# Layer 2's output projection and gate: high weights against high and low activations in one 512-column product, and a new order of the program

## The chip, the cores and the metric

The kernel runs on one core of a Trainium2 chip. The metric is the device time of one execution in microseconds (us). The engines are TensorE (PE), VectorE (DVE), ScalarE (ACT), GpSimd (POOL) and SyncE (SP), which issues most DMAs.

## The reference

Two residual layers over one sequence of T = 256 tokens with D = 1024 channels. Layer 1 mixes tokens by MoBA attention, layer 2 by NSA (compressed, selected and window branches). What surrounds the attention is the same in both, here cut to what matters:

```python
h = rms_norm(x, gain)
q, k, v, z = split(h @ w_in)
o = merge_heads(attention(q, k, v)) * silu(z)
x = x + o @ w_out                                        # output projection: 1024 x 1024
gate = sigmoid(rms_norm(x, ple_gain) @ w_gate)           # gate: 1024 x 1024
x = x + gate * (p @ w_proj)                              # p: 256 channels per token
```

All inputs are float32 and the result has to be as exact as float32 products make it.

## The kernel before

**Products.** x is kept transposed in SBUF as `xT`, 128 channels on the partitions, 8 tiles of channels (k), 256 tokens. Each float32 matrix is split in two fp32r parts, hi and lo, and a product is the sum of three: hi weights with hi activations, hi weights with lo activations, lo weights with hi activations. `split_act` (L498) makes the two parts of an activation tile, ACT the hi part (`ah`), DVE the lo part (`al`), each a tile of its own.

**Units.** Weights come in granules of 128 x 1024 numbers (512 KB): a DMA into `raw`, an ACT copy into `hi` (L494), a DVE subtraction into `lo` (L495). Class `Unit` (L512) covers 512 output columns. For projection, gate and the silu path z, the weights are stationary and the 256 tokens move (`feat`): for each k and each of four 128-row output tiles, three matmuls of 256 columns (`mul`, L531). Two output tiles share one PSUM bank of 512 columns. A granule has two k. Steps are named by layer (n for layer 2), kind, half of the output and granule: `w:no0.1` loads and splits granule 1 of the first half of layer 2's projection, `no0.1` multiplies with it, `no0/0` multiplies the remaining granules for one bank, `no0>0` evacuates that bank.

**Tail.** `tail` (L695) builds these steps for each layer and the evacuations: `add_out` (L725) adds a bank of 512 columns to two tiles of xT with one DVE instruction; `gate` (L731) multiplies by the reciprocal norm (DVE), takes a tanh (ACT), and with two more DVE instructions multiplies by the projected p and adds to xT. In the second half of the gate each output tile has a bank of its own and is evacuated alone (256 columns), the very last in two halves of 128 tokens, each followed by its store.

**Order.** `PROGRAM` (L25) is a string of step names. Class `Plan` (L106) records the instructions of the steps in that order and assigns each engine a static order by list scheduling: the index in the string is the priority, and tables of costs, latencies and a `MARGIN` decide what may go first. All engine instructions are issued by one line of `emit`, so the profile shows nearly every row as L396. Each engine runs its list strictly in that order; a step early in the string can only pass a later one if its inputs come first. The program is: loads of x and the first key weights, layer 1's input products and attention (A, S, T, V steps), its z, projection and gate; then the same for layer 2, whose attention has steps such as `2S0`, `3T3` (softmax and transposes of a head group), `3B` (its masks), `nx.k` (gated attention output, split).

Of the kernel before, what the change touches and what calls it, by code (L numbers as in the profile page):

```python
# [8 lines left out]
F32R = mybir.dt.float32r  # L9
AF = mybir.ActivationFunctionType  # L10
OP = mybir.AluOpType
AX = mybir.AxisListType

P = 128
T = 256
D = 1024
KT = 8
# [2 lines left out]
SWITCH, POW = 150.0, 2300.0  # L20
NRAW, NHI, NLO, NPT, NA = 5, 5, 5, 9, 9
WARM = 16
MARGIN = 100.0

PROGRAM = ("x0 w:c0 x2 c0 x1 w:c1 c1 x3 w:c2 c2 x4 w:c3 w:c4 x5 c3 w:c5 w:k.0 x6 w:c6 consts x7 k.0 w:c7 c4 w:k.1 c5 "  # L25
# [22 lines left out]

STORES = 5

# [8 lines left out]
class View:  # L59


    def __init__(self, tile_, ap, steps=()):
        self.tile, self.ap, self.steps = tile_, ap, steps
# [354 lines left out]
def trunk(ctx: ExitStack, tc: tile.TileContext, a, out):  # L418
# [3 lines left out]
    nc = Plan(tc.nc, {"sb": sb, "psum": psum})  # L422
# [8 lines left out]
    consts, wpool, apool, work = Pool(1), Pool(5), Pool(NA), Pool(2)  # L431
# [8 lines left out]
    xT = consts.tile([P, KT, T], F32, name="xT")  # L440
# [55 lines left out]
        return (hi.rearrange("p (a b) -> p a b", a=shape[0]), lo.rearrange("p (a b) -> p a b", a=shape[0]))  # L496

    def split_act(src, gain=None, either=False):  # L498
        hi = apool.tile([P, T], F32R, tag="ah", name="ah")
        lo = apool.tile([P, T], F32R, tag="al", name="al")  # L500
        if gain is None:
            nc.scalar.activation(hi, src, AF.Copy)
            nc.vector.tensor_tensor(lo, src, hi.bitcast(F32), op=OP.subtract)
        else:
            if either:
                nc.copy(hi, src, gain)
            else:
                nc.scalar.activation(hi, src, AF.Copy, scale=gain)
            nc.vector.scalar_tensor_tensor(lo, src, gain, hi.bitcast(F32), op0=OP.mult, op1=OP.subtract)
        return hi, lo  # L510

    class Unit:  # L512

# [15 lines left out]
            self.w[g] = split(self.src[g], (self.kg, self.n))  # L529

        def mul(self, w, j, k, b, ms=(0, 1), cols=None, parts=(0, 1, 2)):  # L531
            (wh, wl), (xh, xl) = w, self.xs[k]
            first, last = k == 0, k == self.nk - 1
            if self.feat:
                for m in ms:
                    o = self.ps[2 * b + m] if self.apart else self.ps[b][:, m * T:m * T + T]
                    s = slice((2 * b + m) * P, (2 * b + m + 1) * P)
                    nc.tensor.matmul(o, wh[:, j, s], xh, start=first and (self.apart or m == 0), stop=False,
                                     skip_group_check=True)
                    nc.tensor.matmul(o, wh[:, j, s], xl, start=False, stop=False, skip_group_check=True)  # L540
                    nc.tensor.matmul(o, wl[:, j, s], xh, start=False, stop=last, skip_group_check=True)
            else:
                c0, c1 = cols or (0, self.n)
                o, s = self.ps[b][:, c0:c1], slice(b * P, b * P + P)
                for i in parts:
                    x, y = ((xh, wh), (xl, wh), (xh, wl))[i]
                    nc.tensor.matmul(o, x[:, s], y[:, j], start=first and c0 == i == 0, stop=last and i == 2,
                                     skip_group_check=True)
# [12 lines left out]
        def steps(self, name):  # L561

            for g in range(self.granules):
                todo[f"w:{name}.{g}"] = lambda g=g: self.weights(g)
                if g < self.whole:
                    todo[f"{name}.{g}"] = lambda g=g: self.step(g)
            for i in range(len(self.parts)):
                todo[f"{name}/{i}"] = lambda i=i: self.part(i)
            return self

    todo = {}
# [115 lines left out]
    def evac_z(zz, u, i, m, norm):  # L687
        zr = tmp("zr").rearrange("p (a b) -> p a b", a=2)
        nc.vector.tensor_tensor(zr, u.ps[i].rearrange("p (a b) -> p a b", a=2),
                                norm.bc[:, None, :].to_broadcast([P, 2, T]), op=OP.mult)  # L690
        th = tmp("th").rearrange("p (a b) -> p a b", a=2)
        nc.scalar.activation(th, zr, AF.Tanh, scale=0.5)
        nc.vector.scalar_tensor_tensor(flat(zz[:, m:m + 2]), flat(th), 1.0, flat(zr), op0=OP.add, op1=OP.mult)

    def tail(i, oT, pvs, zin, xz, norm, after):  # L695


# [27 lines left out]
        def add_out(u, b, m):  # L725
            nc.vector.tensor_tensor(flat(xT[:, m:m + 2]), flat(xT[:, m:m + 2]), u.ps[b], op=OP.add)

        def split_g(k):
            xg[k] = split_act(xT[:, k], pg[:, i, k:k + 1])

# [19 lines left out]
                    after(k)  # L750

        for h in range(2):
            u = Unit(zin[h], True, xz).steps(f"{n}z{h}")
            for b in range(2):
                todo[f"{n}z{h}>{b}"] = lambda u=u, b=b, m=4 * h + 2 * b: evac_z(zz, u, b, m, norm)
            u = Unit(a["ple_proj"][i, h], True, px, nk=2).steps(f"{n}p{h}")
            for b in range(2):
                todo[f"{n}p{h}>{b}"] = lambda u=u, b=b, m=4 * h + 2 * b: evac_p(u, b, m)
            u = Unit(a["w_out"][i, h], True, xo, close=2).steps(f"{n}o{h}")
            for b in range(2):  # L760
                todo[f"{n}o{h}>{b}"] = lambda u=u, b=b, m=4 * h + 2 * b: add_out(u, b, m)
            u = Unit(a["ple_gate"][i, h], True, xg, apart=h == 1, close=i if h else 2).steps(f"{n}g{h}")
            for j in range(len(u.parts)):
                todo[f"{n}g{h}>{j}"] = lambda u=u, j=j, m=4 * h + (j if h else 2 * j), w=2 - h: gate(u, j, m, w)
# [576 lines left out]
def _arrays(i):  # L1341
    import numpy as np

    def c(v):
        return np.ascontiguousarray(v)
# [31 lines left out]
    r["w1"] = c(i["nsa_cmp_w1"][0].reshape(2, 4, 4, P, 256).transpose(0, 1, 3, 2, 4).reshape(2, 4, P, 1024))  # L1377
    r["w2"] = c(i["nsa_cmp_w2"][0].reshape(2, 2, P, HD).transpose(2, 1, 0, 3))

    r["cst"] = _constants()  # L1380
    return r

# [58 lines left out]
```

## Time and profile before

| | us |
|---|---|
| median of 3 runs | 362.69 (361.23 to 362.87) |
| span of the profiled execution, first to last instruction | 359.3 |
| TensorE busy | 353.5 |
| VectorE busy | 323.9 |
| ScalarE busy | 270.6 |
| GpSimd busy | 29.2 |

The runs' time counts what lies around the span too; for the profiled execution itself only the span is known, and the median of the runs is 3.4 us above it. In a timeline row the columns are the start, the duration, the engine, the line, the operation, out<-in by the program's names (the numbers of buffers left out), the tile and the count of equal instructions drawn together. A PE row's duration includes the time through the array, and its end is modelled, so durations of neighbours overlap; what a product costs on a full PE is the step from its start to the next one's. LDWEIGHTS rows (PEld) run beside the matmul before them.

### The profile page before, as it was taken

What the parts mean: (1) busy time and instruction counts of PE and PEld (TensorE: products, weight loads), DVE (VectorE), ACT (ScalarE), POOL (GpSimd) and SP (SyncE); (2) the same over time, 40 slices, a digit from 0 to 9 for tenths busy, and PEclk for the clock granted to TensorE, in tenths of its full rate; (3) what the DMA queues carried; (4) which work ended last, traced back from release to release, by engine and by line L of the source; (5) the groups of instructions that cost most, each with busy time, mean ns of one, the idle gap of its engine ahead of it and who ended that gap; (6) DMA issues with size and microseconds to landing.
All of it is one profiled execution on the core that took longest, in us unless ns stands there. A gap on an engine that the chain in (4) does not pass through costs nothing.

```text
span 359.3 us, 7138 instructions
## 1 busy us (share of the span) xinstructions
PE 353.5 (98%) x2569; PEld 321.3 (89%) x2569; DVE 323.9 (90%) x799; ACT 270.6 (75%) x592; POOL 29.2 (8%) x26
## 2 busy tenths in 40 slices
PE   8999999999999999999999999999999999999995
PEld 6788888888999999999889998777998999999995
DVE  5999999999999975969999999989999999967965
ACT  5756699986999855937665699959978989956711
POOL 1034004300000000000003300003000000000010
PEclk9999999999999999999999999999999999999999
DMA  7987656433564353645643645177374333142112
GB/s 241 386 313 244 188 186 224 166 117 108 191 193 130 116 177 98 218 153 177 205 141 113 210 120 174 60 291 280 133 232 150 119 126 111 52 146 98 59 31 88
DMA packets 20771, 58.97 MB, mean 164 GB/s; under 512 B 2560, under 2 KB 6016, under 8 KB 20736
## 3 DMA queue, kind: packets, MB, share of 16 engines
q1 hardware_dynamic: 20160, 58.04, 48.9%
q10 hardware_dynamic: 576, 0.48, 0.4%
q8 instruction: 20, 0.33, 0.4%
q14 instruction: 15, 0.12, 0.1%
HBM read 57.46 MB, written 1.05 MB: 163 GB/s over the span
## 4 chain that ended last, share of the span: by engine, by line
PE 96%; DMA 2%; DVE 0%; SPq 0%; issue 0%; ACT 0%; DVEq 0%; ACTq 0%
PE mm L396 74%; PE tr L396 13%; PE s L396 10%; DMA tmp<-in_moba_in 1%; DMA gain_in<-in_gain_in 1%; DVE tmp L396 0%; SPq L396 0%; DVE hi L396 0%; ACT tmp L396 0%; DVEq L1436 0%; DVE xT L396 0%; ACTq L396 0%
## 5 line engine op out<-in xcount | busy, mean ns | idle before, releaser
L396 ACT ACTIVATE hi<-raw 128x1024 fp32r<-128x1024 f32 (+2 forms) x100 | 99.0, 1006 | 29.8 <-PE mm L396 22.3
L396 DVE TENSOR_TENSOR lo<-raw,hi 128x1024 fp32r<-128x1024 f32 (+2 forms) x100 | 115.1, 1159 | 5.5 <-ACT hi L396 4.5
L396 PE MATMUL mm<-al,hi 128*128 128x256 f32 x416 | 116.9, 287 | 0.0
L396 PE MATMUL mm<-ah,lo 128*128 128x256 f32 x416 | 114.5, 286 | 0.0
L396 PE MATMUL mm<-ah,hi 128*128 128x256 f32 x416 | 114.3, 286 | 0.0
L396 PEld LDWEIGHTS mm<-al,hi 128*128 128x128 f32 x416 | 79.3, 191 | 0.2
L396 PEld LDWEIGHTS mm<-ah,lo 128*128 128x128 f32 x416 | 78.0, 191 | 0.3
L396 PEld LDWEIGHTS mm<-ah,hi 128*128 128x128 f32 x416 | 77.8, 191 | 0.4 <-issue 0.2
L396 PE MATMUL mm<-hi,ah 128*128 128x512 f32 (+2 forms) x178 | 66.7, 379 | 0.5 <-ACT ah L396 0.4
L396 PE MATMUL mm<-hi,al 128*128 128x512 f32 (+2 forms) x178 | 66.1, 374 | 0.0
L396 PE MATMUL mm<-lo,ah 128*128 128x512 f32 (+2 forms) x178 | 63.8, 375 | 0.0
L396 ACT ACTIVATE sm<-sm,nb 128x128 f32<-128x128 f32 (+1 forms) x96 | 42.6, 446 | 6.6 <-DVE nb L396 6.2
L396 PEld LDWEIGHTS mm<-hi,ah 128*128 128x128 f32 x178 | 33.4, 188 | 6.4 <-DVE hi L396 0.7
L396 PEld LDWEIGHTS mm<-hi,al 128*128 128x128 f32 x178 | 33.4, 188 | 5.4 <-DVE al L396 0.2
L396 PEld LDWEIGHTS mm<-lo,ah 128*128 128x128 f32 x178 | 33.1, 188 | 5.4 <-DVE lo L396 0.3
L396 DVE CUSTOM_DVE_ANT_0 sm<-s,cst,nr_q 128x128 f32<-128x128 f32 (+1 forms) x96 | 36.2, 410 | 1.6 <-PE s L396 1.3
L396 ACT ACTIVATE pt<-tr 128x384 f32<-128x384 f32 x48 | 21.6, 482 | 3.9 <-PE tr L396 3.6
L396 PE MATMUL tr<-cst,sm 128*128 128x128 f32 x144 | 23.9, 274 | 0.0
L396 POOL TENSOR_TENSOR r_q<-r,neg_half 128x16 f32<-128x16 f32 x5 | 15.8, 3150 | 76.9 <-DVE r L396 76.9
L396 ACT ACTIVATE tmp<-tmp 128x512 f32<-128x512 f32 (+3 forms) x22 | 11.2, 517 | 13.6 <-DVE tmp L396 13.5
L396 PEld LDWEIGHTS tr<-cst,sm 128*128 128x128 f32 x144 | 17.1, 140 | 2.0 <-issue 0.4
L396 ACT ACTIVATE ah<-xT,gain_in 128x256 fp32r<-128x256 f32 x31 | 14.8, 499 | 4.8 <-DVE xT L396 3.7
(176 smaller groups left out, 535.0 us busy)
## 6 DMA issues: line engine op xcount, KB each, us to landing
raw<-in_moba_in SPq DMA_DIRECT2D x28, 512.0 KB, 4.4
raw<-in_nsa_in SPq DMA_DIRECT2D x24, 512.0 KB, 3.7
raw<-in_w_out SPq DMA_DIRECT2D x16, 512.0 KB, 3.5
raw<-in_ple_gate SPq DMA_DIRECT2D x16, 512.0 KB, 3.9
raw<-in_w SPq DMA_DIRECT2D x8, 512.0 KB, 4.1
raw<-in_ple_proj SPq DMA_DIRECT2D x4, 512.0 KB, 4.1
raw<-in_nsa_vs SPq DMA_DIRECT2D x4, 304.0 KB, 2.8
xT<-in_x SPq DMA_DIRECT2D x8, 128.0 KB, 3.8
```

The source lines that it names most:

```text
L396: getattr(getattr(self.nc, o.engine), o.method)(*[real(x) for x in o.args], **{k: real(x) for k, x in o.kwargs.items()})
```

## The change

`split_act` now makes one tile `a` with both parts side by side, 512 columns. A new class `Wide` covers 256 output columns, two output tiles with a bank each, in two granules of four k. Per k and output tile it issues one matmul of the hi weights with all 512 columns, whose left half gets hi x hi and right half hi x lo, and one of the lo weights with the hi part, 256 columns, into the left half. The evacuations sum the halves: `add_wide` does two DVE additions per tile, `gate_wide` an ACT copy of the right half and a DVE addition ahead of the former four instructions. Layer 2's projection (`no0`, `no1`) and gate (`ng0`, `ng1`) use it; the last two tiles (`ng1b`) keep three products of 256 columns. The amount of weights, their granules' size and their splits are as before. `PROGRAM` is written anew for both layers. A version of z's evacuation for this form (`evac_wz`) is added and not used.

```diff
+WIDE, NARROW = "no0 no1 ng0 ng1", "ng1b"
...
-PROGRAM = ("x0 w:c0 x2 c0 x1 w:c1 c1 x3 w:c2 c2 x4 w:c3 w:c4 x5 c3 w:c5 w:k.0 x6 w:c6 consts x7 k.0 w:c7 c4 w:k.1 c5 "
+PROGRAM = ("x0 w:c0 c0 w:k.0 x1 x3 w:c1 x2 w:c2 w:c3 x4 k.0 x6 consts tq a.1 x5 a.3 w:c4 w:c5 c1 w:c6 c2 x7 w:c7 w:k.1 a.5 "
...
     def split_act(src, gain=None, either=False):
-        hi = apool.tile([P, T], F32R, tag="ah", name="ah")
-        lo = apool.tile([P, T], F32R, tag="al", name="al")
+        both = apool.tile([P, 2, T], F32R, tag="a", name="a")
+        hi, lo = both[:, 0], both[:, 1]
...
-        return hi, lo
+        return hi, lo, both.rearrange("p a b -> p (a b)")
...
+    class Wide:
...
+        def mul(self, g, m):
+            (wh, wl), s, o = self.w[g], slice(m * P, m * P + P), self.ps[m]
+            for j in range(4):
+                k = 4 * g + j
+                xh, xl, both = self.xs[k]
+                if self.wide:
+                    nc.tensor.matmul(o, wh[:, j, s], both, start=k == 0, stop=False, skip_group_check=True)
+                else:
+                    nc.tensor.matmul(o[:, :T], wh[:, j, s], xh, start=k == 0, stop=False, skip_group_check=True)
+                    nc.tensor.matmul(o[:, :T], wh[:, j, s], xl, start=False, stop=False, skip_group_check=True)
+                nc.tensor.matmul(o[:, :T], wl[:, j, s], xh, start=False, stop=k == KT - 1, skip_group_check=True)
...
+        def add_wide(u, b, m):
+            for c in (slice(0, T), slice(T, 2 * T)):
+                nc.vector.tensor_tensor(xT[:, m], xT[:, m], u.ps[b][:, c], op=OP.add)
+
+        def gate_wide(u, b, m):
+            ps, x, last = u.ps[b], xT[:, m], i == 1 and m == KT - 1
+            gr, th = tmp("gr")[:, :T], tmp("th")[:, :T]
+            for c, d in (((slice(0, P), slice(T, T + P)), (slice(P, T), slice(T + P, 2 * T))) if last
+                         else ((slice(0, T), slice(T, 2 * T)),)):
+                if u.wide:
+                    nc.scalar.activation(gr[:, c], ps[:, d], AF.Copy)
+                    nc.vector.tensor_tensor(gr[:, c], gr[:, c], ps[:, c], op=OP.add)
+                nc.vector.tensor_tensor(gr[:, c], gr[:, c] if u.wide else ps[:, c], n1.bc[:, c], op=OP.mult)
+                nc.scalar.activation(th[:, c], gr[:, c], AF.Tanh, scale=0.5)
+                nc.vector.scalar_tensor_tensor(th[:, c], th[:, c], 1.0, pp[:, m, c], op0=OP.add, op1=OP.mult)
+                nc.vector.tensor_tensor(x[:, c], x[:, c], th[:, c], op=OP.add)
```

What the change does to the order of the instructions, at three places. First PE in the last head groups of layer 2's attention, before: `tr<-cst,sm` are transposes of softmax tiles, `mm` are weight products.

```order
L396 MATMUL mm_79<-al_114,hi_126 128x256
L396 MATMUL tr_75<-cst_65,pc_192 128x128 x2
L396 MATMUL mm_79<-ah_105,lo_131 128x256
L396 MATMUL tr_76<-cst_65,sm_72 128x128 x3
L396 MATMUL mm_80<-al_115,hi_126 128x256
L396 MATMUL mm_80<-ah_113,lo_131 128x256
L396 MATMUL mm_80<-al_115,hi_126 128x256
L396 MATMUL mm_80<-ah_113,lo_131 128x256
L396 MATMUL mm_80<-ah_105,hi_126 128x256
```

The same engine in the same place of the attention now, where the projection's pairs stand (`a` holds both parts of a split activation):

```order
L397 MATMUL mm_79<-a_108,lo_122 128x256
L397 MATMUL mm_79<-a_113,hi_117 128x512
L397 MATMUL mm_79<-a_113,lo_122 128x256
L397 MATMUL mm_79<-a_109,hi_117 128x512
L397 MATMUL tr_75<-cst_65,sm_71 128x128 x3
L397 MATMUL mm_79<-a_109,lo_122 128x256
L397 MATMUL mm_79<-a_107,hi_117 128x512
L397 MATMUL tr_76<-cst_65,sm_72 128x128 x3
L397 MATMUL mm_79<-a_107,lo_122 128x256
```

Three products of 256 columns have become one of 512 and one of 256. The last softmax transpose had 294 matmuls behind it on PE and has 271 now, 99 of them of 512 columns (of 2413 and 2301 in all). Behind the last masked score row, DVE had 66 instructions and has 104.

Second, SP's queue of loads at the start of the program, before (`xT` is a tile of x, `tmp` and `raw` are weights):

```order
L396 DMA xT_63<-in_x 128x256
L396 DMA tmp_82<-in_moba_in 128x256
L396 DMA xT_63<-in_x 128x256 x3
L396 DMA tmp_85<-in_moba_in 128x512
L396 DMA xT_63<-in_x 128x256
L396 DMA tmp_86<-in_moba_in 128x512
```

and now:

```order
L397 DMA xT_63<-in_x 128x256
L397 DMA tmp_82<-in_moba_in 128x256
L397 DMA raw_124<-in_moba_in 128x1024
L397 DMA xT_63<-in_x 128x256 x3
L397 DMA tmp_85<-in_moba_in 128x512
L397 DMA tmp_86<-in_moba_in 128x512
```

A granule of 512 KB has moved ahead of the second to fourth tile of x.

Third, the end of PE's list now, the last tile but one and the start of the last:

```order
L397 MATMUL mm_81<-a_106,hi_114 128x512
L397 MATMUL mm_81<-a_106,lo_119 128x256
L397 MATMUL mm_81<-a_110,hi_114 128x512
L397 MATMUL mm_81<-a_110,lo_119 128x256
L397 MATMUL mm_79<-a_111,hi_115 128x256 x2
L397 MATMUL mm_79<-a_111,lo_120 128x256
```

The last tile's products are three of 256 columns each, 24 in all, as they were; the tile ahead of it is a wide one.

More of the change, by code (lines that the diff above doesn't have):

```diff
@@ L531, in mul @@
         def mul(self, w, j, k, b, ms=(0, 1), cols=None, parts=(0, 1, 2)):
-            (wh, wl), (xh, xl) = w, self.xs[k]
+            (wh, wl), (xh, xl, _) = w, self.xs[k]
             first, last = k == 0, k == self.nk - 1
@@ L568, in steps, with __init__, weights @@
                 todo[f"{name}/{i}"] = lambda i=i: self.part(i)
+            return self
+    class Wide:
+        def __init__(self, src, xs, wide=True):
+            self.src, self.xs, self.w, self.ps, self.wide = src, xs, {}, None, wide
+        def weights(self, g):
+            if self.ps is None:
+                self.ps = [bank("mm", 4) for _ in range(2)]
+            self.w[g] = split(self.src[g], (4, T))
+        def mul(self, g, m):
[9 more added lines that the diff above has]
+                nc.tensor.matmul(o[:, :T], wl[:, j, s], xh, start=False, stop=k == KT - 1, skip_group_check=True)
+        def steps(self, name):
+            for g in range(2):
+                todo[f"w:{name}.{g}"] = lambda g=g: self.weights(g)
+                for m in range(2):
+                    todo[f"{name}.{g}{m}"] = lambda g=g, m=m: self.mul(g, m)
             return self
@@ L693, in evac_z, with evac_wz @@
         nc.vector.scalar_tensor_tensor(flat(zz[:, m:m + 2]), flat(th), 1.0, flat(zr), op0=OP.add, op1=OP.mult)
+    def evac_wz(zz, ps, m, norm):
+        zr, th = tmp("zr")[:, :T], tmp("th")[:, :T]
+        nc.scalar.activation(zr, ps[:, T:], AF.Copy)
+        nc.vector.tensor_tensor(zr, zr, ps[:, :T], op=OP.add)
+        nc.vector.tensor_tensor(zr, zr, norm.bc, op=OP.mult)
+        nc.scalar.activation(th, zr, AF.Tanh, scale=0.5)
+        nc.vector.scalar_tensor_tensor(zz[:, m], th, 1.0, zr, op0=OP.add, op1=OP.mult)
     def tail(i, oT, pvs, zin, xz, norm, after):
@@ L726, in add_out, with wide @@
             nc.vector.tensor_tensor(flat(xT[:, m:m + 2]), flat(xT[:, m:m + 2]), u.ps[b], op=OP.add)
+        def add_wide(u, b, m):
[13 more added lines that the diff above has]
+                nc.vector.tensor_tensor(x[:, c], x[:, c], th[:, c], op=OP.add)
+                if last:
+                    (nc.scalar if c.start else nc.sync).dma_start(out[:, m, c], xT[:, m, c])
+            if not last:
+                after(m)
+        def wide(kind, h, xs, evac):
+            name = f"{n}{kind}{h}"
+            if name not in WIDE.split():
+                return False
+            for q in range(2):
+                u = Wide(a["w_" + name][q], xs, name + "ab"[q] not in NARROW.split()).steps(name + "ab"[q])
+                for b in range(2):
+                    todo[f"{name}{'ab'[q]}>{b}"] = lambda u=u, b=b, m=4 * h + 2 * q + b: evac(u, b, m)
+            return True
         def split_g(k):
@@ L752, in tail @@
         for h in range(2):
-            u = Unit(zin[h], True, xz).steps(f"{n}z{h}")
-            for b in range(2):
-                todo[f"{n}z{h}>{b}"] = lambda u=u, b=b, m=4 * h + 2 * b: evac_z(zz, u, b, m, norm)
+            if not wide("z", h, xz, lambda u, b, m: evac_wz(zz, u.ps[b], m, norm)):
+                u = Unit(zin[h], True, xz).steps(f"{n}z{h}")
+                for b in range(2):
+                    todo[f"{n}z{h}>{b}"] = lambda u=u, b=b, m=4 * h + 2 * b: evac_z(zz, u, b, m, norm)
             u = Unit(a["ple_proj"][i, h], True, px, nk=2).steps(f"{n}p{h}")
@@ L758, in tail @@
                 todo[f"{n}p{h}>{b}"] = lambda u=u, b=b, m=4 * h + 2 * b: evac_p(u, b, m)
-            u = Unit(a["w_out"][i, h], True, xo, close=2).steps(f"{n}o{h}")
-            for b in range(2):
-                todo[f"{n}o{h}>{b}"] = lambda u=u, b=b, m=4 * h + 2 * b: add_out(u, b, m)
+            if not wide("o", h, xo, add_wide):
+                u = Unit(a["w_out"][i, h], True, xo, close=2).steps(f"{n}o{h}")
+                for b in range(2):
+                    todo[f"{n}o{h}>{b}"] = lambda u=u, b=b, m=4 * h + 2 * b: add_out(u, b, m)
+            if wide("g", h, xg, gate_wide):
+                continue
             u = Unit(a["ple_gate"][i, h], True, xg, apart=h == 1, close=i if h else 2).steps(f"{n}g{h}")
@@ L1378, in _arrays @@
     r["w2"] = c(i["nsa_cmp_w2"][0].reshape(2, 2, P, HD).transpose(2, 1, 0, 3))
+    w = {}
+    for l, (n, z, lo) in enumerate((("", i["moba_w_in"][0], 3072), ("n", i["nsa_w_in"][0], 2608))):
+        w[n + "z"], w[n + "o"] = z[:, lo:lo + D], (i["moba_w_out"], i["nsa_w_out"])[l][0]
+        w[n + "g"] = i["ple_w_gate"][l]
+    for name in WIDE.split():
+        v = w[name[:-1]][:, 512 * int(name[-1]):][:, :512]
+        r["w_" + name] = c(v.reshape(2, 4, P, 2, T).transpose(3, 0, 2, 1, 4).reshape(2, 2, P, 4 * T))
     r["cst"] = _constants()
```

44 rows, old and new, of the table PROGRAM are left out of this document.

## Prediction

> **What bounds the kernel now.** I read the page's busy times first, then the chain of work that ended last, then what TensorE waited for.
>
> ```profile
> span 359.3 us, 7138 instructions
> PE 353.5 (98%) x2569; PEld 321.3 (89%) x2569; DVE 323.9 (90%) x799; ACT 270.6 (75%) x592; POOL 29.2 (8%) x26
> PE 96%; DMA 2%; DVE 0%; SPq 0%; issue 0%; ACT 0%; DVEq 0%; ACTq 0%
> PE tr L396 <- DVE ones L396: 1.1, 1, 1.1
> PE mm L396 <- ACT ah L396: 0.4, 1, 0.4
> ```
>
> TensorE (PE) is busy 353.5 of 359.3 us, 96% of the chain is PE, and in the whole span PE waits measurably twice, both before 6.5 us. So only two things can move the time: what PE has to issue, and whether the other engines still keep up. For the second, a table of stretches: PE, weight loads, VectorE (DVE), ScalarE (ACT), GpSimd, granted clock, DMA share.
>
> ```profile
> core 0: us, PE busy (x) PEld busy (x) DVE busy (x) ACT busy (x) POOL busy (x), PEclk, DMA share, GB/s
> 4.20:11.00 6.80, 6.31 (x30) 4.61 (x30) 6.05 (x14) 4.78 (x11) 0.00 (x0) 1.00 1.00 336
> 120.00:160.00 40.00, 40.00 (x345) 39.12 (x344) 30.40 (x58) 24.16 (x47) 0.70 (x1) 1.00 0.50 158
> 267.00:314.00 47.00, 47.00 (x402) 44.56 (x402) 46.09 (x161) 43.89 (x124) 0.30 (x2) 1.00 0.35 118
> 320.00:355.00 35.00, 35.00 (x302) 34.28 (x297) 26.62 (x48) 16.33 (x29) 1.61 (x1) 1.00 0.19 62
> ```
>
> Two regimes are to be seen. In layer 2's attention (267 to 314) DVE is busy 46.09 of 47.00 us and ACT 43.89: PE, DVE and ACT finish together, and nothing is spare. In the closing stage (320 to 355: output projection and gate) DVE has 8.4 us to spare and ACT 18.7. The granted clock is 1.00 everywhere, so it plays no part.
>
> The runs' median, 362.69, is 3.4 us above this span; I make the sum on the span and add 3.4 at the end.
>
> **What the pairs save.** Each weight tile of these units went through three 256-column products; now a 512-column and a 256-column one. Their price on a full PE is the step from start to start:
>
> ```profile
> 213.40 0.28 PE L396 MATMUL mm<-ah,hi 128*128 128x256 f32 x1
> 213.52 0.28 PE L396 MATMUL mm<-al,hi 128*128 128x256 f32 x1
> 213.64 0.28 PE L396 MATMUL mm<-ah,lo 128*128 128x256 f32 x1
> 213.75 0.28 PE L396 MATMUL mm<-ah,hi 128*128 128x256 f32 x1
> ...
> 64.64 0.39 PE L396 MATMUL mm<-hi,al 128*128 128x512 f32 x1
> 64.86 0.39 PE L396 MATMUL mm<-lo,ah 128*128 128x512 f32 x1
> 65.09 0.28 PE L396 MATMUL mm<-ah,hi 128*128 128x256 f32 x1
> ...
> 217.58 0.28 PE L396 MATMUL mm<-al,hi 128*128 128x256 f32 x1
> 217.70 0.40 PE L396 MATMUL mm<-hi,ah 128*128 128x512 f32 x1
> 217.94 0.65 PE L396 MATMUL mm<-ah,lo 128*128 128x256 f32 x4
> ```
>
> A 256-column product takes 0.12 us, so the three took 0.36 (three steps at 213.40 sum to 0.35, to the rounding). A 512-column product takes 0.22 to 0.24 until the next starts, whether that has 512 columns (64.64 to 64.86) or 256 (64.86 to 65.09, 217.70 to 217.94); a 256-column one ahead of it takes 0.12 as ever (217.58 to 217.70). The pair costs 0.347 to 0.352: its columns are the same 768, and only a fixed cost of one product is gone, about 0.01 us. There are 112 such pairs (eight tiles of the projection and six of the gate's eight, by eight k): **−0.9 to −1.4 us, I take −1.0.** PE issues 112 products fewer, and as many weight loads, which run beside it (34.28 busy of 35.00) and set nothing that these steps don't hold already.
>
> The Trainium skill ("TensorE: Matmul & The Clock Gate", Back-to-back issue gap) gives a sustained 131 ns for a 512-column product, and N/2.4+2.5 ns for an isolated gap, which is an estimated 109 ns for 256 columns and 216 for 512. By the first the pair would save 0.11 us and the change 12 us; the rows' 0.23 side with the second.
>
> **One tile-mode switch fewer.** The new order visits the 64-column value products in seven groups instead of eight; by the steps around the groups in the trace entering and leaving one takes about 0.1 us more on each side. **−0.2 us** (bounds −0.3 to 0).
>
> **The new order, layer 2.** DVE and PE must balance between the compressed values and the last softmax. Before, that stretch of PE's order has 364 products (250 of 256 columns, 14 of 512, 52 transposes, 48 of the 64-column groups), 47 us at the steps above. After, the same softmax work stands in a stretch of 275 (154 of 256, 18 of 512, 54 transposes, the same 48): 96 × 0.12 less, 4 × 0.23 and 2 × 0.1 more, so 10.4 us less: 36.6 of the 47.0. Those weight products now stand behind the attention. DVE loses there: four 1024-column weight subtractions, four 512-column and nine 256-column operations and three small ones, and gains two casts of 0.3:
>
> ```profile
> L396 DVE TENSOR_TENSOR lo<-raw,hi 128x1024 fp32r<-128x1024 f32 x88 | 106.5, 1219 | 5.3 <-ACT hi L396 4.5 <-PE mm L396 0.4
> L396 DVE TENSOR_TENSOR tmp<-mm,bc 128x512 f32<-128x512 f32 x14 | 9.6, 684 | 0.3 <-PE mm L396 0.2
> L396 DVE TENSOR_TENSOR al<-big,ah 128x256 fp32r<-128x256 f32 x16 | 6.2, 415 | 0.3
> ...
> 312.68 1.21 DVE L396 TENSOR_TENSOR lo<-raw,hi 128x1024 fp32r<-128x1024 f32 x1
> 313.82 0.16 DVE L396 RECIPROCAL l<-l 128x4 f32<-128x4 f32 x1
> ```
>
> Neighbours overlap by 0.07 (1.21 long, next start after 1.14), so the steps are 1.14, 0.61 and 0.34: 4 × 1.14 + 4 × 0.61 + 9 × 0.34 + 0.2 − 0.6 = 9.7; some of the nine are scalar operations at 0.27, hence about 9.3. DVE's 46.1 busy become 36.8, plus up to 0.9 us of its own idle time (47.00 − 46.09). So DVE ends 0.2 to 1.1 us behind PE by this sum, and running sums of both orders from the start of the program, with each kind at its mean step, put it at up to 2.4. Every such microsecond is a PE wait: the first product that needs the split attention output, or a late softmax transpose, stands with the whole projection queued behind it. ACT loses the four weight copies too and is no nearer its limit than before. **I take +0.7 us (0 to 2.4),** near the direct count.
>
> "Perfetto Trace Analysis" of the Trainium skill (Optimization Strategy) says to interleave stretches whose most contended engines differ. This order does the opposite; the idle 8.4 us of DVE at 320 to 355 beside 0.9 at 267 to 314 agree with the rule. It changes no number above.
>
> **Layer 1.** The same sums put one shortage of a few tenths at the end of layer 1's attention (around 117 to 122 us of PE work), where the trace has DVE at 30.40 of 40.00 just behind. **+0.2 (0 to 0.5).**
>
> **The start.** Behind the first weights SP's queue now has a 512 KB weight transfer ahead of the next three x tiles. At 336 GB/s (row 4.20:11.00) it puts 1.6 us between them.
>
> ```profile
> GB/s 0 0 0 0 0 14 165 143 223 296 335 270 263 321 348 369 365 290 321 352 382 369 331 300 341 338 335 191 259 294 348 331 369 355 389 386 413 379 388 398
> ...
> 5.43 0.63 PE L396 MATMUL mm<-lo,ah 128*128 128x256 f32 x4
> 6.50 0.73 PE L396 MATMUL mm<-hi,ah 128*128 128x512 f32 x2 [0.43 <-ACT ah L396]
> L396 ACT ACTIVATE hi<-raw 128x1024 fp32r<-128x1024 f32 x88 | 91.1, 1054 | 26.1 <-PE mm L396 20.3 <-issue 1.7 <-ACT tmp L396 1.0
> ```
>
> Before, the four products from 5.43 fill 0.48 us and the next starts at 6.50, 0.6 late; with smaller gaps up to 10 us, counted the same way, PE waits about 1.2. After, the 1.18 MB queued up to and with that transfer land about 5.9 by the rates of the first 12 us (the row of 40 slices, 0.3 us each), ACT needs 1.05 for the copy, and PE goes on near 7.05: 1.1 us of waiting in one piece, and then 18 products of 512 columns (4.1 us) already have their weights. **0 (−1.1 to +0.6).**
>
> **The end.** The evacuations of the wide units are smaller and more: DVE gets some 24 more operations of 256 columns in place of 512-column ones, about 5.6 us more in sum at the 0.34 steps, and ACT seven more. They stand beside the closing products, where DVE has 8.4 of 35 us free. The gate's scale (the transposed reciprocal norm) now stands 15.4 us of PE work before the end instead of 9.7, so evacuation starts earlier. The last tile is still a three-product one evacuated in two 128-column halves, as here:
>
> ```profile
> 354.81 0.28 PE L396 MATMUL s<-ah,lo 128*128 128x256 f32 x1
> 355.12 0.49 DVE L396 TENSOR_TENSOR tmp<-s,bc 128x128 f32<-128x128 f32 x2 [0.20 <-PE s L396]
> ...
> 356.78 0.35 ACTq L396 DMA_DIRECT2D out<-xT  x1
> ```
>
> From the last product's start to the span's end 4.5 us remain the same unless the second-last tile's rows are late: it has its four DVE rows (4 × 0.42) and two ACT rows (0.41) in the 2.9 us of the last tile's 24 products. **0 (0 to +0.5).** Without that cover it would cost those rows, 2.5 us.
>
> **Sum:** −1.0 − 0.2 + 0.7 + 0.2 + 0 + 0 = −0.3 on the span: 359.0, and **362.4** on the scale of the runs.
>
> **Rivals.**
> - *Faster:* PE doesn't wait in layer 2, pairs save all of 1.4, and the start loses its waits: −1.4 − 0.2 − 1.1 = −2.7, 360.0. For it: the direct count's lower end is close to nothing, and the start has the waits to lose. Against it: DVE at 46.09 of 47.00 leaves no slack to be wrong by. Chance 0.22.
> - *Slower:* in layer 2's attention DVE is the bound. It decides from the point where the PE work there (36.6 us) is shorter than DVE's by more than the 1.2 us that pairs and switch save; at the running sums' 2.4, with 0.5 in layer 1 and 0.6 at the start: −1.2 + 3.5 = +2.3, 365.0. For it: both sums point this way and ACT is at 93% too. Against it: the schedule before balanced them within 0.9 us. Chance 0.2.
> - *The change does more than its columns say:* a fixed cost per weight load, not the columns, sets a product's step, and a 512-column one costs little over 0.12. 112 × about 0.1 = −12, 350.5. That is what the 131 ns of the Trainium skill's page named above would mean. Against it stand three rows at 0.23. Chance 0.02.
> - *It doesn't do what it says:* accumulating 256 columns onto half of a bank that a 512-column product has just filled makes PE stand after each pair, by 0.01 or more: the saving is gone, +0.7, 363.4. Three products in a row onto one region at 0.12 speak against it. It lies within the forecast's own band, in its 0.56.
>
> **The numbers.** Forecast 0.56, faster 0.22, slower 0.20, the 12 us 0.02. The range takes in both bounded rivals and a few tenths of rounding: **359.7 to 365.4**. A measurement of this kernel can tell about 0.5% (1.8 us) from no change. Faster by more: the rival's 0.22, the 0.02, and 0.03 of the forecast's lower edge, 0.27; slower by more: 0.20 and 0.01, 0.21; within: 0.52.
>
> **What would show it.** Wide pairs with steps 0.23 and 0.12 at the projection and gate confirm the first term. PE's waits on DVE (a softmax transpose, or the first projection product) between 280 and 306 us should sum to 0.7; zero makes the faster rival, over 2 the slower. PE should wait about 1.1 us once before 7.1. The last product should start about 4.5 us before the end. I am wrong if PE's idle time between 20 us and the last product exceeds 3 us, or if the pair's steps are below 0.33 or above 0.37.

## The result and the profile after

The changed kernel takes **366.13 us** (median of 4 runs, 365.34 to 366.57), the kernel before on the same chip 362.14 (361.23 to 362.87). The ratio of the runs is **1.0117, 95% interval 1.0096 to 1.0138**, some 4 us slower. The prediction, 362.4 with a range up to 365.4, was wrong: it forecast no measurable change.

The page of the changed kernel, the lines that answer to those of before, and then TensorE's waits:

```profile
span 364.1 us, 6947 instructions
PE 354.9 (97%) x2457; PEld 317.3 (87%) x2457; DVE 330.1 (91%) x824; ACT 272.2 (75%) x599; POOL 30.7 (8%) x26
PE 89%; DVE 5%; POOL 2%; DMA 2%; ACT 2%; issue 0%; SPq 0%; DVEq 0%
PE tr L397 <- DVE k L397: 2.1, 1, 2.1
PE mm L397 <- ACT hi L397: 1.2, 1, 1.2
PE tr L397 <- DVE ones L397: 1.1, 1, 1.1
PE mm L397 <- DVE a L397: 0.2, 1, 0.2
PE s L397 <- DVE nb L397: 0.2, 1, 0.2
```

The chain is no longer 96% PE: GpSimd (POOL) is in it with 2%, an engine that is busy for 8% of the span. The first row of the waits is new: one wait of 2.1 us of key transposes for `k`. Stretches of the changed kernel (PE, weight loads, DVE, ACT, POOL, clock, DMA):

```profile
80.00:100.00 20.00, 17.86 (x149) 16.25 (x149) 16.90 (x34) 12.46 (x22) 6.42 (x1) 1.00 0.39 128
280.00:300.00 20.00, 20.00 (x173) 18.34 (x170) 19.91 (x84) 19.52 (x64) 0.15 (x1) 1.00 0.09 27
310.00:320.00 10.00, 10.00 (x81) 8.26 (x80) 10.00 (x24) 8.25 (x18) 0.00 (x0) 1.00 0.21 59
```

PE loses 2.1 us between 80 and 100, in layer 1, where POOL has a single instruction of 6.42 us. In layer 2's attention DVE is full (19.91 of 20.00, 10.00 of 10.00), as forecast, but PE still doesn't wait. The chain around the loss, in order of time (start, duration, what):

```profile
84.84 1.19 DVE ssq L397 x2
86.03 0.20 DVE tq L397
86.22 0.29 DVE r L397 x2
86.51 0.07 issue
86.58 6.43 POOL r_k L397
93.01 0.02 issue
93.04 0.70 DVE k L397
93.74 0.04 issue
93.78 0.55 PE tr L397 x3
```

This is the normalisation of the second half of layer 1's keys: DVE sums squares and scales (`r`), GpSimd raises 128x16 numbers to the power −1/2 (`r_k`), DVE multiplies `k` by it, PE transposes it. DVE's own timeline there:

```profile
86.14 0.36 DVE L397 TENSOR_SCALAR r<-ssq,e 128x8 f32<-128x8 f32 x2
86.41 1.43 DVE L397 TENSOR_TENSOR tmp<-k,tk 128x256 f32<-128x256 f32 x4
87.75 1.29 DVE L397 TENSOR_TENSOR k<-k,tk 128x512 f32<-128x512 f32 x2
88.95 1.29 DVE L397 TENSOR_TENSOR k<-k,tmp 128x512 f32<-128x512 f32 x2
93.04 1.29 DVE L397 TENSOR_TENSOR k<-k,r_k 128x512 f32<-128x512 f32 x2 [2.80 <-POOL r_k L397]
```

While `r_k` lasts, DVE runs eight instructions without a break until 90.24, then has nothing to do for 2.80 us. The 6.42 us of `r_k` are those 3.66 us of DVE work and 2.76 us behind them. In the kernel before, where other work stands around the same chain, the same operation takes 3.00:

```profile
68.72 0.42 DVE L396 TENSOR_TENSOR tmp<-k,tk 128x256 f32<-128x256 f32 x1
68.90 3.00 POOL L396 TENSOR_TENSOR r_k<-r,neg_half 128x16 f32<-128x16 f32 x1 [8.03 <-DVE r L396]
69.23 0.29 DVE L396 CAST qk<-hl 64x256 fp32r<-64x256 f32 x1
```

There DVE pauses for 0.1 us at 69.14, 0.24 behind the start of `r_k`, and 0.24 + 2.76 is 3.00. So the theory: GpSimd's work does not start while DVE runs such instructions back to back, and the new order has put that chain where nothing breaks DVE's run.

What "such" means is seen in the changed kernel itself, at the `r_k` of its first key half:

```profile
38.44 2.90 POOL L397 TENSOR_TENSOR r_k<-r,neg_half 128x16 f32<-128x16 f32 x1 [2.63 <-DVE r L397]
...
38.27 1.41 DVE L397 TENSOR_TENSOR tmp<-mm,tk 128x256 f32<-128x256 f32 x4
39.60 0.68 DVE L397 TENSOR_TENSOR k<-k,tmp 128x512 f32<-128x512 f32 x1
40.20 0.68 DVE L397 TENSOR_TENSOR k<-mm,tk 128x512 f32<-128x512 f32 x1
```

DVE's run is as unbroken there, and `r_k` takes 2.90 us. The difference is that DVE then reads `mm`, which lies in PSUM, where the later half reads `k` and `tk`, both in SBUF. The five such powers of 128x16 numbers that are released beside `tmp<-mm` take 2.90 or 2.91 us in the kernel before, and the five of the changed kernel too.

### The profile page after: what moved, and what is told of

It is laid out like the page before. It is cut to its first block, busy times and chain, and to the rows that moved or that the text cites. A ratio compares the mean times of both kernels' runs of the same rounds, so it can differ in the third digit from the quotient of the medians.

```text
span 364.1 us, 6947 instructions
## 1 busy us (share of the span) xinstructions
PE 354.9 (97%) x2457; PEld 317.3 (87%) x2457; DVE 330.1 (91%) x824; ACT 272.2 (75%) x599; POOL 30.7 (8%) x26
## 3 DMA queue, kind: packets, MB, share of 16 engines
HBM read 57.46 MB, written 1.05 MB: 161 GB/s over the span
## 4 chain that ended last, share of the span: by engine, by line
PE 89%; DVE 5%; POOL 2%; DMA 2%; ACT 2%; issue 0%; SPq 0%; DVEq 0%
PE mm L397 70%; PE tr L397 11%; PE s L397 7%; POOL r_k L397 2%; DMA raw<-in_moba_in 2%; DVE lo L397 1%; DVE sm L397 1%; DVE tmp L397 1%; ACT hi L397 1%; DVE kd_0r L397 0%; DVE hl L397 0%; DVE v_1r L397 0%; ACT kd_0r L397 0%; DVE ssq L397 0%; ACT v_1r L397 0%
## 5 line engine op out<-in xcount | busy, mean ns | idle before, releaser
L397 PE MATMUL mm<-a,hi 128*128 128x256 f32 (+1 forms) x752 | 161.3, 304 | 0.2 <-DVE a L397 0.2
L397 PEld LDWEIGHTS mm<-a,hi 128*128 128x128 f32 x752 | 121.0, 191 | 5.4 <-DVE a L397 0.4
L397 PE MATMUL mm<-a,lo 128*128 128x256 f32 x432 | 120.0, 285 | 0.0
L397 PE MATMUL mm<-hi,a 128*128 128x512 f32 (+2 forms) x356 | 102.8, 378 | 1.2 <-ACT hi L397 1.2
L397 PEld LDWEIGHTS mm<-a,lo 128*128 128x128 f32 x432 | 81.2, 190 | 0.7 <-issue 0.2
L397 PEld LDWEIGHTS mm<-hi,a 128*128 128x128 f32 x356 | 64.1, 191 | 12.3 <-ACT hi L397 1.5
L397 PE MATMUL mm<-lo,a 128*128 128x512 f32 (+2 forms) x178 | 64.2, 377 | 0.0
L397 PEld LDWEIGHTS mm<-lo,a 128*128 128x128 f32 x178 | 33.3, 191 | 5.4
L397 ACT ACTIVATION_READ_ACCUMULATOR sm<-sm,nb 128x1 f32 x96 | 18.3, 191 | 0.0
L397 DVE TENSOR_SCALAR sm<-sm,l 128x128 f32<-128x128 f32 (+1 forms) x68 | 18.0, 311 | 0.1
```

What stands on the lines that cost most here:

```text
L397: getattr(getattr(self.nc, o.engine), o.method)(*[real(x) for x in o.args], **{k: real(x) for k, x in o.kwargs.items()})
```

## Experiments

All ratios are to the kernel before, run again beside each kernel on the same chip, with 95% intervals. Kernels whose other lists are unchanged can be compared with the changed one product by product.

**One short DVE instruction more.** The order stays that of the changed kernel; one instruction is added as it is issued:

```diff
+        if not is_q and evacuated:                 # in rope, behind turn(0, 0)
+            nc.extra = len(nc.ops) - 1
...
         for i in order:                            # in emit
...
+            if i == self.extra:
+                early, ones = (self.tags[t]["real"][0][:, :2] for t in ("early", "ones"))
+                self.nc.vector.tensor_copy(early, ones)
```

> The changed kernel with one DVE instruction more and every list of instructions otherwise as it is: a copy of 128x2 numbers (one SBUF input) behind the first `tmp<-k,tk` of the second key half, where GpSimd's `r_k` is released. In the changed kernel `r_k` took 6.42 us there, 3.66 of it beside eight DVE instructions without a gap that all read two SBUF tensors, and PE waited 2.1 us for `k`. Theory A: GpSimd can't start while DVE runs instructions with two SBUF inputs back to back, and one with a single input lets it in: `r_k` takes 2.9 to 3.2 us, PE's wait for `k` falls to under 0.3, the time falls by 2.0 to 3.5 us against the changed kernel (span 360.6 to 362.1). Theory B: `r_k` is slow by itself at this place, or the order has too few products ahead of the key transposes: `r_k` stays over 5 us and the span within 0.7 of 364.

Measured: 1.0054 (1.0033 to 1.0075). PE's wait for `k` is gone, and `r_k` lasts 3.03 us:

```profile
86.57 3.03 POOL L397 TENSOR_TENSOR r_k<-r,neg_half 128x16 f32<-128x16 f32 x1 [7.15 <-DVE r L397]
...
86.40 0.42 DVE L397 TENSOR_TENSOR tmp<-k,tk 128x256 f32<-128x256 f32 x1
86.74 0.20 DVE L401 COPY early<-ones 128x2 f32<-128x2 f32 x1
86.85 1.08 DVE L397 TENSOR_TENSOR tmp<-k,tk 128x256 f32<-128x256 f32 x3
```

Product by product this kernel stands level with the changed one from 15 to 90 us (within 0.03), is 2.41 us ahead at 100 and 2.80 at 130: an instruction that takes 0.1 us of DVE saves 2.8. Theory B has fallen.

**The same with two inputs,** `tensor_tensor(early, ones, ones, op=OP.add)` in place of the copy.

> As the kernel with the copy, but the added DVE instruction is an addition of 128x2 numbers, with two SBUF inputs. If it is the second input that keeps GpSimd out (theory A), `r_k` stays at 5 to 6.5 us, PE still waits 2 us for `k`, and the span stays at 363.5 to 364.8. If any short instruction makes the gap, `r_k` takes about 3 us here too and the span falls as with the copy. Theory B: no change in either.

Measured: 1.0023 (1.0006 to 1.0040), `r_k` 3.03 us again. This part of theory A fell: a second input in SBUF alone doesn't keep GpSimd out when the instruction is short. It takes the unbroken run of long ones; that these must have both inputs in SBUF is what the `r_k` at 38.44 speaks for, and no experiment changed the inputs of the long ones. From 90 to 130 us the gain on the changed kernel is 2.8 us again (1.03 to 3.82). The span is 1.9 us under that of the kernel with the copy, though their lists differ in nothing else: 1.0 us at the start, where ACT could copy the first key granule at 6.31 instead of 7.35 us, and the rest around 245 us, where the other waited 0.3 us for a `raw<-in_w` transfer and for what followed. Single executions stand that far apart by their transfers.

**The same copy six instructions later** (behind the second `k<-k,tk`).

> The changed kernel with the same short copy, but six DVE instructions later, behind the second `k<-k,tk`. It came out that any short DVE instruction lets GpSimd in, with one or two inputs, so the theory now is: `r_k` starts at the first break in DVE's run of long instructions and then takes 2.8 us. The copy stands about 2.4 us behind the release of `r_k`, so `r_k` lasts 5.1 to 5.4 us (3.03 with the early copy, 6.42 without), PE waits for `k` 0.6 to 1.1 us, and the span is 362.2 to 363.2, between the two. Rival: the copy helps by its place in the order or by chance, and `r_k` is 3.0 or 6.4.

Measured: 1.0081 (1.0050 to 1.0111), span 362.2, PE's wait for `k` 0.9:

```profile
85.86 5.22 POOL L397 TENSOR_TENSOR r_k<-r,neg_half 128x16 f32<-128x16 f32 x1 [7.15 <-DVE r L397]
...
87.04 1.28 DVE L397 TENSOR_TENSOR k<-k,tk 128x512 f32<-128x512 f32 x2
88.24 0.18 DVE L401 COPY early<-ones 128x2 f32<-128x2 f32 x1
88.34 1.28 DVE L397 TENSOR_TENSOR k<-k,tmp 128x512 f32<-128x512 f32 x2
91.12 1.29 DVE L397 TENSOR_TENSOR k<-k,r_k 128x512 f32<-128x512 f32 x2 [1.50 <-POOL r_k L397]
```

The copy stands 2.4 us behind the start of `r_k`, and 2.4 + 2.8 is 5.2. With the three places (0.2, 2.4 and 3.7 us until the first break, which is a pause or a short instruction; 3.03, 5.22 and 6.42 us) the rule holds to 0.1 us. Of the 1.9 us by which the span is under that of the changed kernel, the key transposes give 1.2; 0.7 are there by 20 us already, and are luck at the start.

**The pairs undone in the new order.**

```diff
-WIDE, NARROW = "no0 no1 ng0 ng1", "ng1b"
+WIDE, NARROW = "no0 no1 ng0 ng1", "no0a no0b no1a no1b ng0a ng0b ng1a ng1b"
...
-            for c in (slice(0, T), slice(T, 2 * T)):
+            for c in (slice(0, T), slice(T, 2 * T))[:1 + u.wide]:
```

> The changed kernel with its new order, but every wide unit issues three products of 256 columns and is evacuated without the second half. It undoes the pairs alone. By the steps of the pair (0.35 against 0.36 us, 112 times) PE's work grows by 1.1 us and the time by 1.1; where the shorter evacuation matters (fewer DVE and ACT instructions in the last 50 us), less, down to 0. If the pairs were what made the change slower, the time falls.

Measured: 1.0145 (1.0115 to 1.0175), 0.28% or 1.0 us more than the changed kernel, its span 1.1 us more. The intervals of the two ratios overlap, so the times alone don't tell them apart. The traces do: from the last `mm<-raw,big` product, ahead of all the pairs, to the start of the last product it is 107.0 us here and 105.9 in the changed kernel. The pairs save what their steps say.

**The start, twice.** First the old start in `PROGRAM`, which makes the schedule anew:

```diff
-PROGRAM = ("x0 w:c0 c0 w:k.0 x1 x3 w:c1 x2 w:c2 w:c3 x4 k.0 x6 consts tq a.1 x5 a.3 w:c4 ...
+PROGRAM = ("x0 w:c0 x2 c0 x1 w:c1 c1 x3 w:c2 c2 x4 w:c3 w:c4 x5 c3 w:c5 w:k.0 x6 w:c6 consts x7 k.0 tq a.1 a.3 ...
```

> The changed kernel with the steps of the start as before (up to the first granule of the key weights), the rest in the new order. Theory: the 512 KB granule ahead of three x tiles made PE stand from 6.9 to 8.4 us; with the old start PE's first 512-column product comes at 6.5 instead of 8.4 and the time falls by 1.0 to 1.6 us. Rival: the wait only moves to later products of the start (before, they waited at 6.5, 9.8 and 10.1 us), and the time changes by less than 0.5 us. As the schedule behind it is made anew, the later waits can shift by some tenths.

Measured: 1.0215 (1.0172 to 1.0258), with times from 366.54 to 370.64: a miss. In its profiled execution the first 20 us do lose 1.2 us less (PE's starts beyond their usual steps sum to 1.6 us instead of 2.8), but the remade schedule stands 1.1 us at 107.7, 0.7 at 120.9 and 1.5 at 123.2. It tells nothing of the start's price. So only the first key granule was moved, every other list kept:

```diff
-    nc.emit(order)
+    nc.emit(nc.late(order, at))    # steps w:k.0 and k.0 behind those of w:c2 and c2, on each engine
```

> The changed kernel with every engine's list as it is, but the instructions of the first key granule (its load, its ACT copy, its DVE subtraction, its 18 products of 512 columns and their kind) moved behind those of the third weight step of the start. Theory: its 512 KB, queued ahead of three x tiles, keep PE from 5.8 or 6.8 until 8.4 us; moved, PE's first 512-column product comes at 6.4 to 6.8, waits of the first 20 us fall from 2.8 to 1.5 to 1.9 us, and the time falls by 0.9 to 1.4 us (span 362.7 to 363.3). Rival: the transfers are the bound of the start, the wait only moves to other products, and the time changes by less than 0.4 us.

Measured: 1.0096 (1.0072 to 1.0120), within the intervals of the changed kernel; span 362.6. The granule's wait is smaller, and another has come:

```profile
6.87 0.94 PE L418 MATMUL mm<-hi,a 128*128 128x512 f32 x3
8.32 0.50 PE L418 MATMUL mm<-lo,a 128*128 128x512 f32 x1 [0.52 <-DVE lo L418]
```

In this execution it was 0.76 us ahead of the changed kernel at 20 us; in the next one, with the same start, 0.02. The kernels with an unchanged start scatter as far: level, 1.0 and 0.7 ahead in the three with an added instruction. Against the usual steps, PE has lost 1.4 to 2.8 us by 25 us in six kernels with the new start, and 1.6 to 2.3 in four with the old one, so a price of the new start over some tenths isn't shown. One part is the granule's: both kernels with the late granule, and none of the others, gain 0.3 us on the changed kernel at 41.7 to 42.1 us.

**Both, late granule and copy.**

> Both: the key granule moved behind the third weight step, and the short DVE copy behind the first `tmp<-k,tk` of the second key half. If the two are the causes and add up, the span is 364.1 less 2.6 less 1.0 to 1.3, 360.2 to 360.5, and the time against the kernel before 0 to +0.4%. If small waits elsewhere in the new order grow when the large ones go, it stays above 361.

Measured: 1.0018 (1.0002 to 1.0034), span 360.8. The copy gives its 2.8 us here too (0.35 ahead of the changed kernel at 90 us, 3.14 at 130). The two edits add up nearly: the span is 360.8 and was expected at 360.2 to 360.5.

**Halves of the program exchanged.** Steps up to the last evacuation of layer 1's attention (`E3`) from one order, the rest from the other; schedules are made anew.

```diff
-PROGRAM = new
+PROGRAM = old[:old.index("E3") + 1] + [t for t in new if t not in old[:old.index("E3") + 1]]
```

> The changed kernel's code (pairs, one tile for both parts) with the steps in the old order up to the last evacuation of layer 1's attention, and in the new order from there. The schedule is made anew from this list. If the loss lies in layer 1's half and the second half is worth its pairs, the span is 358 to 359.5, within 0.3% of the kernel before or faster by up to 0.4%. If the second half loses too (DVE short in layer 2's attention, as the prediction had it), 359.7 to 361.

Measured: **0.9972 (0.9955 to 0.9988), 360.99 us: faster than both kernels.** Its span was 359.3, and past the warm-up PE has no wait in the view:

```profile
PE tr L396 <- DVE ones L396: 1.1, 1, 1.1
...
69.60 3.01 POOL L396 TENSOR_TENSOR r_k<-r,neg_half 128x16 f32<-128x16 f32 x1 [8.02 <-DVE r L396]
...
280.00:300.00 20.00, 20.00 (x176) 18.78 (x176) 19.84 (x82) 19.83 (x60) 0.15 (x1) 1.00 0.22 62
```

The whole loss is in the order of layer 1's half: 1.0117 with it, 0.9972 without.

> Layer 1's half in the old order and the second half in the new one, with the pairs undone (three products of 256 columns, evacuated without the second half). It tells what is left of the second half's gain. If the pairs are all of it, the time rises by 1.0 us against the kernel with pairs, to the kernel before within 0.3%. If the new order of the second half gives the gain, it stays 0.2 to 0.3% under the kernel before; if that order costs something that the pairs pay for, it is over 0.3% slower.

Measured: 1.0003 (0.9985 to 1.0022). Undoing the pairs takes the gain away, 0.31% or 1.1 us; the new order of the second half is worth nothing that can be told, either way.

> The reverse: the kernel before (three products, two tiles for the parts), with the steps in the new order up to the last evacuation of layer 1's attention and in the old order from there. If layer 1's half holds the loss, the span is 363.5 to 366 with a GpSimd `r_k` of about 6.4 us and PE's wait for `k` of about 2 us; if the second half holds it, 359 to 360.5.

Measured: 1.0410 (1.0386 to 1.0435), far beyond both expectations. `r_k` lasts 6.42 us here too and PE waits 2.1 us for `k`, with the old code for products; that much confirms the place. The other 10 us are stalls that this mixed list makes itself, such as this one in layer 1's output projection, and nothing more is read from it:

```profile
152.33 0.74 PE L393 MATMUL mm<-ah,hi 128*128 128x256 f32 x4 [1.43 <-ACT ah L393]
```

## Why the prediction was wrong, by its steps

**The pairs: right.** In the changed kernel they take 0.23 and 0.11 to 0.12 us:

```profile
330.00 0.39 PE L397 MATMUL mm<-a,hi 128*128 128x512 f32 x1
330.24 0.27 PE L397 MATMUL mm<-a,lo 128*128 128x256 f32 x1
330.35 0.40 PE L397 MATMUL mm<-a,hi 128*128 128x512 f32 x1
330.58 0.28 PE L397 MATMUL mm<-a,lo 128*128 128x256 f32 x1
330.70 0.39 PE L397 MATMUL mm<-a,hi 128*128 128x512 f32 x1
```

That is 0.35 a pair, −1.0 us as taken; the two kernels without pairs lose 1.0 and 1.1 us by their times and 1.1 and 0.9 by the traces. The rival of a 12 us gain is out, and so is the one in which PE stands after each pair.

**One tile-mode switch fewer, −0.2:** the changed kernel's trace has the seven groups of 64-column products, and their steps in and out are 0.1 us longer as before; the saving was not measured by itself.

**Layer 2's attention, +0.7: not there.** DVE was as full as the sum had it, but finished in time: the view has no wait of PE behind 200 us at all. The lower bound of zero was the right end. The deficit came out of two sums of 37 us each at mean steps and was no larger than what such sums can be wrong by; the running sums' 2.4 was further off.

**Layer 1, +0.2: this step failed.** The prediction applied "the same sums" of DVE's work to layer 1 and found a few tenths at the end of its attention. A shortage of that size is there: at 121.2 us a score product starts 0.3 late, behind DVE's `nb`. But it was taken for all that layer 1 could lose. The sums hold busy times only. They do not hold a chain that passes through a third engine: DVE, then GpSimd, then DVE, then PE. GpSimd, busy for 8% of the span, got no term, and its durations were not looked at by place. The runs put 2.8 us there: 2.4 at the transposes, and 0.4 behind them at 105.7 to 106.5, where PE waits for DVE's `a`; both go with the early copy. The trace of before has a sign of that price:

```profile
56.73 4.14 POOL L396 TENSOR_TENSOR r_q<-r,neg_half 128x16 f32<-128x16 f32 x1 [20.15 <-DVE r L396]
...
56.90 1.22 DVE L396 TENSOR_TENSOR lo<-raw,hi 128x1024 fp32r<-128x1024 f32 x1
58.15 0.69 DVE L396 TENSOR_TENSOR hl<-tr,hl 64x512 fp32r<-64x512 f32 x1
```

Here DVE's run ends at 58.12, 1.39 us behind the start, and 1.39 + 2.75 is the 4.14; what follows is both a pause of 0.03 us and an instruction that reads `tr` in PSUM, and which of them let GpSimd in is not shown. Against the 3.00 of `r_k` that asked for an explanation, and the new list has eight long DVE instructions in a row behind `r`, all with both inputs in SBUF.

**The start, 0 (−1.1 to +0.6):** a wait of one piece came, at 8.40 instead of 7.05, because the granule was there at 7.29 and not at 5.9. By 5.9 us the queues had moved 1.2 MB (206 GB/s), as the forecast had it, but the granule was not complete, so transfers issued behind it must have had a part of the rate. Against the spread of the same start in other kernels, 1 us, the term is neither confirmed nor refuted.

**The end, 0: right.** The last product starts at 359.69 and 4.4 us follow, as before (4.5).

**The sum:** −1.1 for the pairs and +2.8 for `r_k` make 1.7 of the 4.2 us that the ratio says; 2.5 are left, all in layer 1's half. The traces place most of the rest. From 146.7 us on the changed kernel issues the same 1544 products as the kernel with the old first half, and it is 4.9 us behind there and 4.8 at the end. Of the 4.9, 0.6 are lost by 25 us, 2.7 with `r_k`, and 1.1 by products that start 0.2 to 0.3 us late at about 42, 61.0, 110.0 and 121.2 us, where the other kernel has no such late start; 0.5 are not placed. Why the engines ahead of these small late starts are late in the new order was not settled.

Neither of the two signs that the prediction gave for being wrong came: PE's idle time between 20 us and the last product is 2.87 us and not over 3, and the pair's step is 0.35. A row of 256 columns is 0.28 long at steps of 0.12, so a product that starts a tenth late leaves no idle time, and the idle sum misses part of the loss.

The slower rival had the sign, and the wrong place and mechanism: its 365.0 us came from DVE in layer 2.

## What to carry to other kernels

- Before an order is judged by sums per engine, follow each chain that leaves the saturated engines, however idle the third engine is, and count from its trace what it takes at each place, not on average.
- Where a GpSimd result is waited for, look at what DVE runs behind its release: here a row of long instructions with both inputs in SBUF delayed it by the row's length, and one short instruction right there ended the wait.
- When a schedule is remade, an experiment on one part changes others; adding an instruction to the finished lists kept the stretch ahead of it level to 0.03 us, and showed an effect that times alone would have blurred.

## What was not expected of the hardware

**GpSimd waits for a break in DVE's run.** Behind a run of long instructions with both inputs in SBUF, a power of 128x16 numbers takes about 2.8 us from the first break, and its profiled duration includes the time until then. The Trainium skill ("SBUF — State Buffer", SBUF: two separate sides) describes an exclusive lock on a shared port pair between GpSimd and DVE instructions with two SBUF inputs, where whoever comes first blocks the other. The runs agree that DVE's run keeps GpSimd out, and that a run which reads PSUM doesn't (2.90 us at 38.44); they differ in that a short instruction with two such inputs lets it in as well, and that DVE isn't slowed while `r_k` works: its 512-column operations keep their 0.6 us steps in the kernel with the early copy.

**The full rate of the first products comes at a time that varies.** All executions warm PE up with the same 16 transposes from 1.05 us on, at 0.21 us each. The step falls to 0.11 or 0.12 at about 3.8 us in the kernel before, 4.7 and 4.1 with the copy and the addition, 6.4 with the old start; in the changed kernel the first 12 products, until 6.8, keep the step of 0.21, while the profile shows a granted clock of 1.00 throughout. "TensorE: Matmul & The Clock Gate" of the Trainium skill (Part 1: The HAM clock gate) gives a free-running window of about 3.4 us for this; the spread here is some 3 us. It cost nothing where PE waited for a load behind these products anyway. In the kernel with the old first half PE waited for no load there; the slow step lasted until 7.1 us, and the first 512-column product came at 7.09, against 6.50 in the kernel before.
